# The order list of latent attention extended over the first part of the joining stage

## The chip, the cores and the metric

The kernel runs as one program on one core of a Trainium2 chip. The figure of merit is the device time of one execution in microseconds (us). The kernel before was timed three times: 1685.85, 1685.1 and 1686.39 us, median 1685.85. A further execution was recorded by the hardware profiler, and every duration below comes from that one recording. The engines are named as in the profile: PE (matrix products), PEld (its weight loads), DVE (vector), ACT (scalar), POOL (general purpose, here mostly the issuer of stores) and SP (issuer of most loads). L12 is line 12 of the kernel that is spoken of; the changed kernel's lines from 917 on have other numbers.

## The reference

One step of an encoder layer, for a prompt of 1024 rows and a sample of 32 rows that also sees a cache of 512 rows, at a width of 1024:

```
h = rms_norm(x) * (1 + scale1) + shift1
q-latent, kv-latent, rope key, SB q/k/v, gate A, gate B = split(h @ w_in)
o_A = mla_attend(...)        # latent attention, 8 heads of 64, softmax, block-causal mask of 64 rows
o_B = sb_attend(...)         # stick-breaking attention, 8 heads of 64
merged = sigmoid(gate A) * (o_A @ w_proj_a) + sigmoid(gate B) * (o_B @ w_proj_b)
x = x + gate1 * rms_norm(merged @ w_out)
x = x + gate2 * rms_norm(conv_ffn(rms_norm(x) * (1 + scale2) + shift2))
```

The change concerns the end of `mla_attend` and the beginning of `o_A @ w_proj_a` in `merged`.

## The kernel before

**Precision.** Each fp32 operand of a large product is cut into a high and a low part. `hi` (L68) writes the high part on ACT, `lo` (L71) subtracts it on DVE, and `mm3` (L75, L76, L77) issues three matmuls for each product: high by high, high by low, low by high.

**Stages.** Normalised input, combined projection, stick-breaking attention, latent attention, joining (`merged` and `w_out`), and the feed-forward part follow each other. All activations are kept transposed, so that a tile has 128 features as partitions and up to 1056 rows (1024 and 32) as columns.

**Latent attention.** The eight heads are treated as four pairs, 0 to 3. For each head there are four units of 256 query rows, each with two blocks of 128 rows. Scores go into banks `s`, are exponentiated into a tile `A` of 128 x 1056, normalised there, and turned block by block through a bank `tr` into high and low parts: `PTh`/`PTl`, or `ptd` (one fixed pair of tiles) for the diagonal block. The products with the values run into a bank `pv` (L820). Its two halves are copied (`o<-pv` on ACT, L792) and added (`o<-pv,o` on DVE, L794). The outputs of pairs 0 to 2 are stored to `oa` in DRAM and those of pair 3 are split straight into a tile `V`.

**The order list.** What PE, ACT and DVE do in this stage follows a list written out by hand, `ORDER_M`, which `mla_attend` executes token by token. A token's digit is the pair, and its letter the step: S scores, M m n maximum, E exponential, R reciprocal, C or c normalising (DVE or ACT), T turning, h v high and low part of what was turned, V products with the values, o p the copy and the addition of the output, Y one step of the sample's attention, q r the split of pair 3's outputs. In `3T5.2`, 5 is the unit (4 and above: the pair's second head, counted backwards) and 2 the block. Tokens without a digit belong to gate B's projection (`proj_b`): Q e l its operand, U W w its weights, f one product (three matmuls of 264 columns) into a bank `mm`, and G the store of a finished bank, that is an ACT copy to a tile `nat` (L1889) and a transfer issued by POOL into `pbd` in DRAM (L1890). There are 32 such stores. Inside the listed part the three engines keep exactly this order; POOL and SP are not in the list and issue their transfers in an order that the scheduler derives.

**After the list.** The rows of pairs 1, 2 and 0 are loaded back from `oa` into tiles `big` (L1678, SP) and split into `QH`/`QL`, `KH`/`KL`, `QH`/`QL`. The weights for the joining stage's first two feature tiles (m = 0 and 1) are loaded and split, fifteen products with pairs 1, 2 and 0 run into five banks (m = 0 into mm, mm, s and m = 1 into s, s), and an ACT instruction on one column calls for the sigmoid's table (L1694), placed behind the last exponential. These steps are outside the list, so the scheduler puts them among and behind the list's last tokens. The fourth part of these products (pair 3, tile `V`) and everything else of the joining stage follows in `stage_merge`, which loads gate rows (`t<-gd` L2004, `t<-pbd` L2010) and `w_out` (L2027).

**Tile slots.** A tile of a tag is taken from a ring of a few buffers. Who writes a tile waits until the buffer's earlier reader is done, so an ACT copy into `nat` waits until the transfer that reads the same buffer has landed.

Of the kernel before, what the change touches and what calls it, by code (L numbers as in the profile page):

```python
# [17 lines left out]
P = 128  # L18
D = 1024
KT = 8  # L20
TP = 1024
TS = 32
T = TP + TS
NB = 352
PAST = 512
KS = PAST + TS
# [6 lines left out]
BIG = 1056  # L33
# [11 lines left out]
class K:  # L45
# [777 lines left out]
    def sb_weights(self, pieces, w):  # L823
# [76 lines left out]
        2v6.0 3n0.0 2c7.0 f 2y 3S1.0 3E0.0 2V6.0 3E0.1 G 2T7.0 3S1.1 f4 3S2.0b 3Y 3R0.0 2H 3c0.0 U 3R0.1 3M1.0  # L900
        3C0.1 2L 3n1.0 3M1.1 2g 2h7.0 2o6 3E1.0 3R1.0 W 3S2.0a 3c1.0 3Y 2v7.0 2p6 2V7.0 2b 3n1.1 3E1.1 3T0.0
        3M2.0b w 3R1.1 3Y 3M2.0a 3m2.0 3h0.0 3Y 2o7 3E2.0a 3S2.1a 3E2.0b G 3C1.1 3v0.0 f 3Y 2p7 3S2.1b 3s2.0 3Y
        3M2.1b 3M2.1a 3V0.0 3m2.1 3Y 3T1.1 3o0 3E2.1b 3T1.0 3h1.1 3h1.0 f 3v1.1 3Y f 3E2.1a f 3v1.0 3Y 3s2.1
        3R2.0 3Y 3S3.0a 3p0 3c2.0 f 3q f2 3V1.1 3R2.1 3S3.0b 3C2.1 3Y 3T2.1 3h2.1 3Y 3M3.0b 3Y f 3S3.1b 3V1.0
        3M3.0a 3m3.0 3Y 3v2.1 3T2.2 3E3.0b 3Y 3S3.1a 3E3.0a 3o1 3Y 3M3.1b 3S4.0b 3h2.2 W 3r 3M3.1a 3m3.1 3E3.1b
        3p1 3v2.2 3Y 3T2.0 w 3S4.0a 3M4.0b 3s3.0 3E3.1a 3R3.0 3S4.1a 3Y 3h2.0 3M4.0a 3m4.0 3s3.1 3c3.0 3E4.0b
        3v2.0 3V2.2 3S4.1b 3V2.1 3R3.1 3C3.1 3q 3T3.3 3Y 3E4.0a G 3T3.2 3V2.0 G 3M4.1b 3M4.1a 3h3.3 3h3.2 3v3.3
        3Y 3m4.1 3r 3s4.0 3T3.1 3o2 3p2 3E4.1a 3v3.2 3E4.1b 3Y 3s4.1 3h3.1 3R4.1 3V3.3 3R4.0 3V3.2 3C4.1 3c4.0
        3v3.1 3q 3Y 3T3.0 3T4.3 3V3.1 3S5.0a 3h3.0 f 3v3.0 3T4.2 3V3.0 3h4.3 3Y 3h4.2 3M5.0a 3v4.3 3o3 3S5.1b
        3T4.1 3S5.0b 3h4.1 3Y 3p3 3v4.2 3M5.0b 3V4.3 f 3Y 3V4.2 3m5.0 3v4.1 f 3r 3E5.0b 3Y 3E5.0a 3T4.0 3S5.1a  # L910
        3M5.1b 3s5.0 3Y 3R5.0 3M5.1a 3h4.0 3S6.1 3m5.1 3Y 3E5.1a 3E5.1b 3c5.0 3v4.0 3Y 3M6.1 3q 3Y 3S6.0 3s5.1
        3S7.1 3R5.1 3n6.1 3E6.1 3C5.1 3T5.2 3h5.2 3M6.0 3n6.0 3Y 3M7.1 3E6.0 3n7.1 3v5.2 3V4.1 3R6.1 3R6.0 3c6.0
        3Y 3C6.1 3V4.0 3T5.1 3o4 3h5.1 3r 3T5.0 3h5.0 3E7.1 f 3p4 3S7.0 3V5.2 3v5.1 3v5.0 G f 3M7.0 3q 3T6.1
        3h6.1 3n7.0 3R7.1 3r 3v6.1 3E7.0 3V5.1 3V5.0 3R7.0 3o5 3T6.0 3h6.0 f2 3c7.0 f 3p5 3C7.1 G 3v6.0 3V6.1
        3T7.0 3h7.0 3V6.0 f 3o6 f 3v7.0 f 3p6 f 3q 3V7.0 3r G 3o7 3p7 3q f3 3r f 3q 3r G
# [240 lines left out]
    def stage_sb(self):  # L1156
# [50 lines left out]
        fill = self.gates()  # L1207
        E = mybir.EngineType
        for p in range(4):
# [203 lines left out]
    def stage_mla(self):  # L1413
        nc, a = self.nc, self.a

        O = self.Op = self.tc.alloc_tile_pool(name="mlo", bufs=2, side="right", reuse_waits="tile")
        M = self.tc.alloc_tile_pool(name="mla", bufs=2, side="right", reuse_waits="tile")
# [7 lines left out]
        K0 = [O.tile([P, T], F32R, name=self.nm(n), bufs=1) for n in ("KH", "KL")]  # L1425
# [152 lines left out]
        raw = load_values(0)  # L1578
# [8 lines left out]
        def key_rows(i):  # L1587
# [20 lines left out]
        o3, sample = [], []  # L1608
# [49 lines left out]
        def shared(k):  # L1658
# [3 lines left out]
                latents.append(self.mla_sample_latents())  # L1662
            next(latents[0])

        E = mybir.EngineType
# [6 lines left out]
        q = lambda: [self.tl(O, [P, T], F32R, g) for g in ("QH", "QL")]  # L1672
        q0, q1 = q(), q()
        self.xh, self.xl = zip(q1, q0, K0, o3)
        ks = (1, 2, 0)
        for k in ks:
            f = self.tl(self.At, [P, BIG], F32, "big")
            nc.sync.dma_start(f, self.oad[k])  # L1678
            self.hi(self.xh[k], f)
            self.lo(self.xl[k], f, self.xh[k])  # L1680
        self.pa = []
        raw = self.tl(M, [P, 2, KS], F32, "KSm")
        raw = [self.w_proj_a(m, raw[:, m, :512]) for m in range(2)] + [self.w_proj_a(2)]
        self.w2 = raw[2]
        for m, tags in enumerate(("mm mm s", "s s")):
            h, l = self.split_proj(raw[m])
            self.pa.append((h, l, [self.bank(g) for g in tags.split()]))
            for ps, (c0, n) in zip(self.pa[m][2], self.BLK[::-1]):
                for k in ks:
                    self.mm3(ps[:, :n], h[:, k], l[:, k], self.xh[k][:, c0 : c0 + n], self.xl[k][:, c0 : c0 + n], k == 1, False)  # L1690

        z = self.tl(self.sm, [P, 1], F32, "ss")
        with self.tc.issue_after(self.exp.ins):
            nc.scalar.activation(z, self.epsc, AF.Sigmoid)  # L1694
        M.release()
        self.Lp.release()
        self.sm3.release()
# [133 lines left out]
    def proj_b(self, M, AB):  # L1831

        nc, a = self.nc, self.a
        HB = HC // 2
        TILES = ((0, 1), (1, 2), (3, 1), (4, 1), (5, 2), (7, 1))
        raw, w, ps, obs, fs, done = [], [], [], [], [], [0, 0, 0, 0, 0]
# [48 lines left out]

        def store():
            m, c0, x = ps.pop(0)
            g = self.tl(self.At, [P, 512], F32, "nat")[:, :HB]
            nc.scalar.copy(g, x)  # L1889
            nc.gpsimd.dma_start(self.pbd[m, :, c0 : c0 + HB], g)  # L1890
# [273 lines left out]
    HB = ((0, 256), (256, 272))  # L2164
# [557 lines left out]
```

## Time and profile before

| | |
|---|---|
| Median of three runs | 1685.85 us (1685.1 to 1686.39) |
| Profiled execution | 1686.9 us, of which the recorded span is 1685.1 us |
| Granted TensorE clock over the span | 0.994 |
| PE busy | 1643.0 us (97%) |
| DVE busy | 1268.6 us (75%) |
| ACT busy | 1008.5 us (60%) |
| POOL busy | 299.7 us (18%) |

Latent attention's pair 3 stands at about 763 to 827 us of the span, and the first products of the joining stage begin at 827.3 us. "Busy" is time in which an engine has an instruction under way; matmuls overlap, so a row of PE may start before the row above has ended. In a timeline row the first number is the start and the second the duration in us, and what stands in brackets is the idle time ahead of the instruction and what ended it. A row with SPq or POOLq is the issue of a transfer and not the transfer.

### The profile page before, as it was taken

The numbers are of one execution on the slowest core, as the hardware profiler recorded it, in microseconds if no ns is written. First come the engines' busy times: TensorE is split into PE (matmuls) and PEld (weight loads), VectorE is DVE, ScalarE is ACT, GpSimd is POOL, SyncE is SP. The second block draws the span as 40 slices with busy tenths as digits, with TensorE's granted clock in tenths as the row PEclk, the third lists the DMA queues.
The fourth block names the chain that finished last, engine by engine and source line by source line (L and its number), as shares of the span: only waits on it lengthen the run. The fifth ranks groups of instructions, "written<-read, shape, count | busy, mean of one in ns | idle before, by whom it ended". The sixth has DMA issues, their size and how long they took to land. (4 is left out here: it accounts for less than half of the span.)

```text
span 1685.1 us, 30257 instructions
## 1 busy us (share of the span) xinstructions
PE 1643.0 (97%) x11592; PEld 1506.5 (89%) x11592; DVE 1268.6 (75%) x2140; ACT 1008.5 (60%) x1945; POOL 299.7 (18%) x581
## 2 busy tenths in 40 slices
PE   5999999999999999999999999999999999999997
PEld 2899999999998889998888799999999999877885
DVE  4865698989883688987766789878777778787455
ACT  4544697878874488887762675545444444454442
POOL 4113312111210221111000222212111112200013
PEclk8999999999999999999999999999999999999999
DMA  9336885566632533222374523333333333797643
GB/s 357 107 108 199 276 250 164 161 193 181 180 117 50 163 99 97 80 88 66 132 235 135 184 88 123 133 127 105 128 126 97 133 129 105 244 325 243 197 140 122
DMA packets 194145, 260.62 MB, mean 155 GB/s; under 512 B 23374, under 2 KB 132304, under 8 KB 193936
## 3 DMA queue, kind: packets, MB, share of 16 engines
q1 hardware_dynamic: 172944, 198.50, 37.8%
q0 software_dynamic: 20688, 59.56, 10.0%
q8 instruction: 91, 1.49, 0.4%
q10 hardware_dynamic: 368, 0.63, 0.1%
q14 instruction: 54, 0.44, 0.1%
HBM read 191.11 MB, written 67.82 MB: 154 GB/s over the span
## 5 line engine op out<-in xcount | busy, mean ns | idle before, releaser
L68 ACT ACTIVATE wh<-wr 128x1024 fp32r<-128x1024 f32 (+2 forms) x151 | 130.1, 864 | 229.2 <-PE s L2176 85.4
L71 DVE TENSOR_TENSOR wl<-wr,wh 128x1024 fp32r<-128x1024 f32 (+2 forms) x151 | 148.3, 985 | 78.6 <-ACT wh L68 78.4
L75 PE MATMUL mm<-hh,wh 128*128 128x352 f32 x456 | 152.3, 334 | 0.4 <-DVE hh L332 0.4
L76 PE MATMUL mm<-hl,wh 128*128 128x352 f32 x456 | 148.1, 325 | 0.4 <-DVE hl L333 0.3
L77 PE MATMUL mm<-hh,wl 128*128 128x352 f32 x456 | 148.1, 325 | 0.0
L2175 PE MATMUL mm<-T,wh 128*128 128x256 f32 (+1 forms) x376 | 108.3, 288 | 0.0
L2177 PE MATMUL mm<-T,wl 128*128 128x256 f32 (+1 forms) x376 | 107.3, 286 | 0.4 <-DVE wl L71 0.2
L2176 PE MATMUL mm<-T,wh 128*128 128x256 f32 (+1 forms) x376 | 106.8, 284 | 0.0
L2175 PE MATMUL s<-T,wh 128*128 128x256 f32 (+1 forms) x348 | 99.4, 286 | 0.0
L2177 PE MATMUL s<-T,wl 128*128 128x256 f32 (+1 forms) x348 | 99.4, 286 | 0.0
L2176 PE MATMUL s<-T,wh 128*128 128x256 f32 (+1 forms) x348 | 98.9, 284 | 0.0
L71 DVE TENSOR_TENSOR wl<-S,wh 128x1024 fp32r<-128x1024 f32 (+1 forms) x55 | 59.2, 1078 | 51.5 <-ACT wh L68 49.9
L75 PEld LDWEIGHTS mm<-hh,wh 128*128 128x128 f32 x456 | 86.3, 189 | 3.8 <-issue 2.1
L76 PEld LDWEIGHTS mm<-hl,wh 128*128 128x128 f32 x456 | 86.4, 190 | 2.3 <-DVE hl L333 0.9
L2316 DVE SCALAR_TENSOR_TENSOR u<-u,c,u 128x1058 f32<-128x1058 f32 x68 | 87.1, 1317 | 1.9 <-ACT u L2313 0.7
L806 PE MATMUL tr<-c,A 128*128 128x128 f32 x576 | 86.7, 272 | 0.0
L77 PEld LDWEIGHTS mm<-hh,wl 128*128 128x128 f32 x456 | 86.1, 189 | 0.6 <-issue 0.4
L68 ACT ACTIVATE wh<-S 128x1024 fp32r<-128x1024 f32 (+1 forms) x55 | 51.8, 943 | 48.2 <-PE s L2176 13.4
L2175 PE MATMUL tr<-T,wh 128*128 128x272 f32 (+1 forms) x272 | 77.9, 287 | 0.0
L2177 PE MATMUL tr<-T,wl 128*128 128x272 f32 (+1 forms) x272 | 77.8, 286 | 0.0
L2176 PE MATMUL tr<-T,wh 128*128 128x272 f32 (+1 forms) x272 | 77.4, 285 | 0.0
L68 ACT ACTIVATE PTh<-tr 128x512 fp32r<-128x512 f32 x96 | 57.0, 599 | 27.3 <-PE tr L806 22.9
(768 smaller groups left out, 5812.0 us busy)
## 6 DMA issues: line engine op xcount, KB each, us to landing
wr<-in_w_up_dram SPq DMA_DIRECT2D x44, 512.0 KB, 4.0
dr<-in_w_down_dram SPq DMA_DIRECT2D x43, 512.0 KB, 5.2
wr<-in_w_in_dram SPq DMA_DIRECT2D x33, 512.0 KB, 6.5
A<-in_w_ada_dram SPq DMA_DIRECT2D x32, 512.0 KB, 5.8
wr<-gdn SPq DMA_DIRECT2D x30, 512.0 KB, 4.4
gdn<-u POOLq DMA_DIRECT2D x23, 512.0 KB, 5.2
gd<-nat POOLq DMA_DIRECT2D x48, 176.0 KB, 3.4
t<-gd SPq DMA_DIRECT2D x16, 528.0 KB, 5.3
```

What stands on the lines that cost most here:

```text
L68: self.nc.scalar.activation(out, in_, AF.Identity, scale=scale)
L71: return self.nc.vector.tensor_tensor(out, full, hi.bitcast(F32), ALU.subtract)
L75: m(ps, lh, rh, start=start, stop=False)
L76: m(ps, lh, rl, start=False, stop=False)
L77: self.pe = m(ps, ll, rh, start=False, stop=stop).ins
L806: self.nc.tensor.transpose(tr[:, (2 * s + q) * P : (2 * s + q + 1) * P], at[q][:, b * P : b * P + P], self.idt)
L2175: m(ps[:, :n], w[0][:, k], x[0][:, k, c], start=first and k == 0, stop=False, skip_group_check=True)
L2176: m(ps[:, :n], w[0][:, k], x[1][:, k, c], start=False, stop=False, skip_group_check=True)
L2177: i = m(ps[:, :n], w[1][:, k], x[0][:, k, c], start=False, stop=k == 3, skip_group_check=True)
L2316: nc.vector.scalar_tensor_tensor(y, u[:, w : w + YW], self.cvT[:, w, cc : cc + 1], y, ALU.mult, ALU.add)
```

## The change

The steps that stood behind the list become tokens of it, under a new digit 7: `7h` and `7l` split the loaded rows (three each), `7W` and `7w` split the joining stage's weights (two each, m = 1 ahead of m = 0), `7P` is one of the fifteen products (fifteen tokens), and `7z` is the one-column sigmoid that calls for the table. The list's part for pair 3 is written anew from `3S1.1` on, with the same steps in another order, and the pair-7 tokens stand in its last part. The products of m = 1 come first and take banks s and s, then m = 0 takes s, mm, mm. The three loads of rows are written where the first `7h` stands. Finally, the last four of the 32 stores of gate B's projection copy into a tile `A` and no longer into a `nat`. The engines execute the same numbers of instructions of every kind as before.

```diff
+        3M7.1 3n7.1 f G 3T6.1 3n7.0 3V5.1 f 7h 7h 7l 7h 3E7.1 3h6.1 f 3E7.0 7l 3V5.0 7P 7l 3o5 3q 3T6.0 3R7.0 G
+        f 3h6.0 f2 7P 3v6.1 3p5 7P 3c7.0 7W 7P 3R7.1 7P 3V6.1 G 3C7.1 3T7.0 3h7.0 3v6.0 7P 3V6.0 7w 3r 7P 7P 3q
+        7P 3o6 3v7.0 3p6 3V7.0 3r 7z 7P 3o7 7P 3q 3p7 3r 7P 7P 7P 3q 3r 7P
...
+        def rows():
+            q = lambda: [self.tl(O, [P, T], F32R, g) for g in ("QH", "QL")]
+            q0, q1 = q(), q()
+            self.xh, self.xl = zip(q1, q0, K0, o3)
+            for k in ks:
+                fs.append(self.tl(self.At, [P, BIG], F32, "big"))
+                nc.sync.dma_start(fs[-1], self.oad[k])
...
+        def merge_weights(i):
...
+            m = 1 - todo[2 + i]
...
+                self.pa[m] = [self.tl(self.W, [P, 1024], F32R, g)[:, :512] for g in ("wh", "wl")]
+                self.hi(self.pa[m][0], raw[m])
...
+            for m, tags in ((1, "s s"), (0, "s mm mm")):
...
+        last = dict(h=lambda: merge_rows(0), l=lambda: merge_rows(1), W=lambda: merge_weights(0), w=lambda: merge_weights(1),
+                    P=lambda: next(products), z=lambda: nc.scalar.activation(self.tl(self.sm, [P, 1], F32, "ss"), self.epsc, AF.Sigmoid))
...
-            self.mla_attend({p: lambda p=p: one(p) for p in range(4)}, {8: second, 9: lambda k: first[k]()}, shared)
+            self.mla_attend({p: lambda p=p: one(p) for p in range(4)},
+                            {7: lambda k: last[k](), 8: second, 9: lambda k: first[k]()}, shared)
...
-        for m, tags in enumerate(("mm mm s", "s s")):
-            h, l = self.split_proj(raw[m])
...
-        with self.tc.issue_after(self.exp.ins):
-            nc.scalar.activation(z, self.epsc, AF.Sigmoid)
...
-            g = self.tl(self.At, [P, 512], F32, "nat")[:, :HB]
+            done[5] += 1
+            g = self.tl(self.At, *(([P, 512], F32, "nat") if done[5] < 29 else ([P, TP], F32, "A")))[:, :HB]
```

In the rows below a name ends in its tile's number, and all numbers of the rewritten part differ between the two kernels.

On ACT, at the end of latent attention before the change, the table load stands directly behind the last exponential, and the splits of loaded rows (`KH<-big`, `QH<-big`) stand between copies and splits of the outputs:

```order
L1694 ACT_TABLE_LOAD
L1694 ACTIVATE ss_1793_10571<-c_4_76 128x1
L792 COPY o_1761_10399<-pv_1757_10364 64x256
L68 ACTIVATE PTh_1763_10406<-tr_1762_10401 128x512
L971 ACTIVATE A_1753_10356<-A_1753_10356,sum_1755_10358 128x128
L1889 COPY nat_1765_10421<-mm_1759_10374 128x264
L68 ACTIVATE KH_1044_6987<-big_1780_10500 128x1056
L68 ACTIVATE ptd_1042_6982<-tr_1767_10430 128x384
L792 COPY o_1769_10443<-pv_1766_10425 64x256
L68 ACTIVATE V_1582_9577<-o_1761_10399 64x256
L68 ACTIVATE QH_1777_10494<-big_1781_10504 128x1056
L1889 COPY nat_1771_10463<-mm_1768_10439 128x264
```

On ACT after the change, at the corresponding place, a store's copy (into `A`) stands ahead of the three row splits, which follow each other, and the last two exponentials (`A,sum<-s,mx,lat`) and another store's copy stand behind them:

```order
L1915 COPY A_1765_10406<-mm_1742_10306 128x264
L68 ACTIVATE QH_1767_10421<-big_1771_10425 128x1056
L68 ACTIVATE KH_1044_6987<-big_1772_10427 128x1056
L68 ACTIVATE QH_1769_10423<-big_1773_10429 128x1056
L963 ACTIVATE A_1760_10382,sum_1762_10384<-s_1763_10385,mx_1761_10383,lat_955_6225 128x256
L68 ACTIVATE ptd_1042_6982<-tr_1766_10409 128x384
L963 ACTIVATE A_1755_10368,sum_1757_10370<-s_1758_10371,mx_1756_10369,lat_955_6225 128x128
L792 COPY o_1776_10452<-pv_1764_10395 64x256
L68 ACTIVATE V_1582_9577<-o_1754_10364 64x256
L1915 COPY A_1780_10463<-mm_1759_10377 128x264
L68 ACTIVATE PTh_1778_10460<-tr_1777_10455 128x512
L972 ACTIVATE A_1755_10368<-A_1755_10368,sum_1757_10370 128x128
```

The row splits moved ahead of the last exponentials, as one block of three, and the two store copies that stand around them use `A` tiles.

Also on ACT after the change, the table load stands nearly at the list's end, between the last two copies of outputs:

```order
L68 ACTIVATE ptd_1042_6982<-tr_1786_10505 128x384
L68 ACTIVATE V_1582_9577<-o_1776_10452 64x256
L792 COPY o_1788_10531<-pv_1784_10496 64x256
L1713 ACT_TABLE_LOAD
L1713 ACTIVATE ss_1790_10541<-c_4_76 128x1
L792 COPY o_1792_10547<-pv_1789_10535 64x256
L68 ACTIVATE V_1582_9577<-o_1788_10531 64x256
L68 ACTIVATE V_1582_9577<-o_1792_10547 64x256
```

It moved behind the copy of the last output but one.

On PE before the change, the joining stage's products (352 columns) begin where the last product of gate B's projection (264 columns) has ended, in banks mm and s:

```order
L75 MATMUL mm_1773_10470<-ObH_1412_8746,wh_1050_6993 128x264
L76 MATMUL mm_1773_10470<-ObL_1413_8747,wh_1050_6993 128x264
L77 MATMUL mm_1773_10470<-ObH_1412_8746,wl_1051_6994 128x264
L75 MATMUL mm_1786_10517<-QH_1775_10492,wh_1784_10513 128x352
L76 MATMUL mm_1786_10517<-QL_1776_10493,wh_1784_10513 128x352
L75 MATMUL s_1788_10519<-QH_1775_10492,wh_1784_10513 128x352
L76 MATMUL s_1788_10519<-QL_1776_10493,wh_1784_10513 128x352
```

On PE after the change the first of these products stands among attention's value products and turnings, with more of both still to come:

```order
L820 MATMUL pv_1764_10395<-PTh_1749_10349,V_1424_8795 128x256
L820 MATMUL pv_1764_10395<-PTl_1750_10350,V_1424_8795 128x256
L75 MATMUL s_1775_10447<-QH_1767_10421,wh_1746_10335 128x352
L76 MATMUL s_1775_10447<-QL_1768_10422,wh_1746_10335 128x352
L77 MATMUL s_1775_10447<-QH_1767_10421,wl_1747_10336 128x352
L806 MATMUL tr_1777_10455<-c_1_70,A_1737_10292 128x128
L806 MATMUL tr_1777_10455<-c_1_70,A_1726_10243 128x128
```

The joining products moved from behind attention's last product to between its turnings and value products. PE's order is the same in both kernels up to about 763 us of the span and again from the place that stood at about 853 us.

More of the change, by code (lines that the diff above doesn't have):

```diff
@@ new lines @@
+        3V0.0 3Y 3s2.0 3M2.1b 3m2.1 3o0 3T1.0 2b 3E2.1b 3T1.1 3E2.1a 3p0 3Y 3h1.1 f 3R2.0 3s2.1 3h1.0 3Y f 3v1.1
+        3R2.1 3c2.0 3C2.1 3V1.1 3Y f 3S3.0b 3v1.0 3T2.2 3Y 3h2.2 3V1.0 3M3.0b 3Y f 3v2.2 3o1 3T2.1 3S3.0a f 3q
+        3Y 3p1 3h2.1 3V2.2 W 3M3.0a 3S3.1b 3m3.0 3Y 3v2.1 3T2.0 3r 3Y 3M3.1b 3E3.0a 3E3.0b 3S3.1a 3S4.0a 3Y
+        3h2.0 3M3.1a 3Y 3m3.1 3M4.0a 3q 3E3.1a 3s3.0 3S4.0b f 3R3.0 3c3.0 3E3.1b 3S4.1b G 3v2.0 3Y 3M4.0b 3m4.0
+        3s3.1 3E4.0a 3R3.1 3E4.0b 3Y 3C3.1 3Y 3S4.1a w 3T3.3 3M4.1b 3V2.1 3h3.3 3M4.1a 3T3.2 3h3.2 3Y 3m4.1
@@ new lines @@
+        3V2.0 3v3.2 3E4.1a 3Y 3o2 3E4.1b 3T3.1 3v3.3 3s4.0 3p2 3r 3h3.1 3V3.3 3S5.1b f 3V3.2 3Y 3v3.1 3s4.1
+        3R4.1 3R4.0 3Y 3T3.0 f 3Y f 3V3.1 3h3.0 3Y 3c4.0 3Y 3C4.1 3S5.0a 3S5.0b 3Y 3q 3v3.0 3M5.0b 3V3.0 3Y
+        3M5.0a 3T4.3 3h4.3 3o3 3m5.0 3Y G 3E5.0b 3M5.1b 3S5.1a 3E5.0a 3v4.3 3T4.2 3p3 3r 3Y 3q 3Y 3M5.1a 3s5.0
+        3m5.1 3S6.1 3h4.2 3r 3v4.2 3V4.3 3R5.0 3E5.1a f 3E5.1b 3Y 3T4.0 3M6.1 3c5.0 3s5.1 3h4.0 3n6.1 3V4.2
+        3R5.1 3T4.1 3S6.0 3C5.1 3E6.1 G 3v4.0 f2 3M6.0 3T5.2 f 3n6.0 3h4.1 f 3E6.0 3h5.2 3R6.1 3v4.1 7W 3V4.1
@@ L1663, in shared, with merge_rows @@
             next(latents[0])
+        ks, fs, raw, self.pa, todo = (1, 2, 0), [], [], [None, None], [0] * 6
+        def rows():
[5 more added lines that the diff above has]
+                nc.sync.dma_start(fs[-1], self.oad[k])
+        def merge_rows(i):
+            if not fs:
+                rows()
+            k, f = ks[todo[i]], fs[todo[i]]
+            todo[i] += 1
+            if i:
+                self.lo(self.xl[k], f, self.xh[k])
+            else:
+                self.hi(self.xh[k], f)
@@ new lines, in merge_weights @@
+        def merge_weights(i):
+            if not raw:
+                x = self.tl(M, [P, 2, KS], F32, "KSm")
+                raw[:] = [self.w_proj_a(m, x[:, m, :512]) for m in range(2)] + [self.w_proj_a(2)]
+                self.w2 = raw[2]
+            m = 1 - todo[2 + i]
+            todo[2 + i] += 1
+            if i:
+                h, l = self.pa[m][:2]
+                self.lo(l, raw[m], h)
+            else:
+                self.pa[m] = [self.tl(self.W, [P, 1024], F32R, g)[:, :512] for g in ("wh", "wl")]
+                self.hi(self.pa[m][0], raw[m])
@@ new lines, in merge_products @@
+        def merge_products():
+            for m, tags in ((1, "s s"), (0, "s mm mm")):
+                h, l = (x.rearrange("p (k c) -> p k c", k=4) for x in self.pa[m])
+                banks = []
+                self.pa[m] = h, l, banks
+                for g, (c0, n) in zip(tags.split(), self.BLK[::-1]):
+                    banks.append(self.bank(g))
+                    for k in ks:
+                        self.mm3(banks[-1][:, :n], h[:, k], l[:, k], self.xh[k][:, c0 : c0 + n], self.xl[k][:, c0 : c0 + n], k == 1, False)
+                        yield
@@ L1665, in stage_mla @@
+        products = merge_products()
+        last = dict(h=lambda: merge_rows(0), l=lambda: merge_rows(1), W=lambda: merge_weights(0), w=lambda: merge_weights(1),
+                    P=lambda: next(products), z=lambda: nc.scalar.activation(self.tl(self.sm, [P, 1], F32, "ss"), self.epsc, AF.Sigmoid))
         E = mybir.EngineType
         with self.tc.manual_schedule(engines={E.PE, E.Activation, E.DVE}):
-            self.mla_attend({p: lambda p=p: one(p) for p in range(4)}, {8: second, 9: lambda k: first[k]()}, shared)
+            self.mla_attend({p: lambda p=p: one(p) for p in range(4)},
+                            {7: lambda k: last[k](), 8: second, 9: lambda k: first[k]()}, shared)
@@ L1668, in stage_mla @@
         for _ in split(self.osm[:, 3], slice(0, P), slice(TP, T)):
             pass
[L1672 to L1682, printed above, removed]
@@ L1683, in stage_mla @@
-        raw = [self.w_proj_a(m, raw[:, m, :512]) for m in range(2)] + [self.w_proj_a(2)]
-        self.w2 = raw[2]
-        for m, tags in enumerate(("mm mm s", "s s")):
-            h, l = self.split_proj(raw[m])
[L1687 to L1690, printed above, removed]
@@ L1835, in proj_b @@
         TILES = ((0, 1), (1, 2), (3, 1), (4, 1), (5, 2), (7, 1))
[L1836 removed]
+        raw, w, ps, obs, fs, done = [], [], [], [], [], [0, 0, 0, 0, 0, 0]
         def fetch():
```

21 lines of the change are left out of this document (4 added, 17 removed).

## The prediction

> **What bounds the kernel now.** I read the page first, for which engine carries the span:
>
> ```profile
> PE 1643.0 (97%) x11592; PEld 1506.5 (89%) x11592; DVE 1268.6 (75%) x2140; ACT 1008.5 (60%) x1945; POOL 299.7 (18%) x581
> ```
>
> PE is busy for 97% of 1685.1 us, and the change neither adds nor removes a matmul. So it can only gain what PE idles in the rewritten stretch. PE's order differs from about 763 us on and is the same again from what stood at 853 us; I therefore asked for busy time by stretches (PE, PEld, DVE, ACT, POOL, then clock and DMA share) and for PE's waits in the same window:
>
> ```profile
> 821.00:827.30 6.30, 5.25 (x39) 4.93 (x40) 5.51 (x10) 5.82 (x12) 1.55 (x10) 1.00 1.02 396
> 827.30:836.00 8.70, 7.56 (x48) 7.26 (x47) 3.37 (x5) 4.33 (x6) 0.54 (x1) 1.00 0.44 160
> ...
> sum 82.20, PE 78.00 PEld 69.76 DVE 60.12 ACT 60.98 POOL 6.91; mean PE 15.60 PEld 13.95 DVE 12.03 ACT 12.20 POOL 1.38
> ```
> ```profile
> PE pv L820 <- DVE o L794: 2.9, 4, 1.1
> PE mm L75 <- ACT nat L1889: 1.1, 1, 1.1
> ```
>
> The five stretches of 764 to 846.2 us add up to 82.20 us, with PE busy for 78.00. The waits have two names only. The timeline of PE shows them one by one, with the idle time in brackets:
>
> ```profile
> 766.98 0.72 PE L820 MATMUL pv<-ptd,V 128*128 128x256 f32 x4 [0.37 <-DVE o L794]
> ...
> 804.18 0.74 PE L820 MATMUL pv<-ptd,V 128*128 128x256 f32 x4 [0.78 <-DVE o L794]
> ...
> 821.34 0.75 PE L820 MATMUL pv<-ptd,V 128*128 128x256 f32 x4 [1.07 <-DVE o L794]
> ...
> 825.26 0.74 PE L820 MATMUL pv<-ptd,V 128*128 128x256 f32 x4 [0.71 <-DVE o L794]
> ...
> 829.27 0.43 PE L75 MATMUL mm<-QH,wh 128*128 128x352 f32 x1 [1.14 <-ACT nat L1889]
> ```
>
> The first value product of a unit needs the only bank `pv` back, which the copy and the addition of the previous output must have read. The idle times are 0.37 + 0.78 + 1.07 + 0.71 + 1.14 = 4.07 us: that is the ceiling, 0.24% of the time. What held them up is seen on ACT and DVE:
>
> ```profile
> 801.40 1.10 ACT L68 ACTIVATE QH<-big 128x1056 fp32r<-128x1056 f32 x1
> 802.38 0.61 ACT L68 ACTIVATE PTh<-tr 128x512 fp32r<-128x512 f32 x1
> 803.02 0.37 ACT L792 COPY o<-pv 64x256 f32<-64x256 f32 x1
> ...
> 818.94 1.28 ACT L1694 ACT_TABLE_LOAD   x1
> 820.23 0.20 ACT L1694 ACTIVATE ss<-c 128x1 f32<-128x1 f32 x1
> 820.46 0.36 ACT L792 COPY o<-pv 64x256 f32<-64x256 f32 x1
> ...
> 828.84 0.38 ACT L1889 COPY nat<-mm 128x264 f32<-128x264 f32 x1 [1.09 <-DMA pbd<-nat]
> ```
> ```profile
> 820.86 0.43 DVE L794 TENSOR_TENSOR o<-pv,o 64x256 f32<-64x256 f32 x1 [1.72 <-ACT o L792]
> ...
> 825.57 1.26 DVE L71 TENSOR_TENSOR QL<-big,QH 128x1056 fp32r<-128x1056 f32 x1
> ```
>
> A row split of 1.10 us stands ahead of the output copy at 803.02, and the table load ahead of that at 820.46. The last wait is another thing: the copy at 828.84 sat 1.09 us until an earlier store out of its `nat` buffer had landed, and PE waited for the bank which that copy empties.
>
> **The change, part by part.** *Removed.* I walked PE, ACT and DVE by hand through the new order with the durations of before's rows. The output copies now stand behind short instructions, and of the five waits 0.15 us remain (the value product near 766 us, whose `ptd` low part is late); the others vanish, with margins of 0.35 us and more. So the full 4.07 us is taken as removed, and what remains or comes new is charged below.
>
> *Table load.* It stands behind the last output copy but one. From the value products that this copy reads to the end of the last unit's, PE has nine joining matmuls at 0.16 us (rows below) and four value products at about 0.12: 1.9 us. In that time ACT copies (0.36) and loads the table (1.28 + 0.20): 1.84, just ready for the last copy. The last copy, the addition (0.43) and the split of the output follow:
>
> ```profile
> 826.53 0.41 ACT L68 ACTIVATE V<-o 64x256 fp32r<-64x256 f32 x1
> ```
> ```profile
> 827.21 0.42 DVE L71 TENSOR_TENSOR V<-o,V 64x256 fp32r<-64x256 f32 x1
> ```
>
> Together 0.36 + 0.43 + 0.41 + 0.42 = 1.6 us, against 18 further joining matmuls (2.9 us) ahead of the first that reads tile V. Nothing is charged; without the nine matmuls the load would cost up to 1.48.
>
> *Moved matmuls.* A product behind a turning costs more than one behind a product:
>
> ```profile
> 756.76 0.60 PE L806 MATMUL tr<-c,A 128*128 128x128 f32 x4
> 757.11 0.37 PE L75 MATMUL mm<-ObH,wh 128*128 128x264 f32 x1
> 757.32 0.28 PE L76 MATMUL mm<-ObL,wh 128*128 128x264 f32 x1
> 757.44 0.28 PE L77 MATMUL mm<-ObH,wl 128*128 128x264 f32 x1
> ```
> ```profile
> 830.98 0.33 PE L75 MATMUL mm<-KH,wh 128*128 128x352 f32 x1
> 831.14 0.32 PE L76 MATMUL mm<-KL,wh 128*128 128x352 f32 x1
> ```
>
> The first takes 757.32 − 757.11 = 0.21 us, the next 0.12, so 0.09 us for each seam. In the changed stretch there were 16 such seams and now there are 19: 3 x 0.09 = 0.27 us lost.
>
> *Row loads, row splits, stores.* Here lies what the new order may cost. POOL issues the sample's rows and the gate stores, SP the loads behind them:
>
> ```profile
> 815.08 0.54 POOL L1811 DMA_DIRECT2D oa<-os  x1 [20.46 <-DVE os L1809]
> 817.70 0.54 POOL L1890 DMA_DIRECT2D pbd<-nat  x1 [2.08 <-ACT nat L1889]
> ```
> ```profile
> 816.88 0.84 SPq L1678 DMA_DIRECT2D big<-oa  x2
> 817.77 0.90 SPq L2004 DMA_DIRECT2D t<-gd  x2
> ```
>
> The rows' load needs the sample's write, 816.88 − 815.08 = 1.8 us later, and the gate rows follow on the same queue. From then on the DMA engines are full: the share in the first row of stretches is 1.02. The store issued at 817.70 meets that, and the next one too. Issue to landing of these transfers, from the DMA views of 817 to 818.5 and 822 to 823 us, then least, median and longest of the four stores of 815 to 831 us, and of the four gate-row loads (528 KB, L2004) issued between 815 and 821 us:
>
> ```profile
> pbd<-nat POOLq DMA_DIRECT2D x1, 132.0 KB, 6.0
> ```
> ```profile
> pbd<-nat POOLq DMA_DIRECT2D x1, 132.0 KB, 6.5
> ```
> ```profile
> DMA to landing us min/median/max: 3.5/5.1/6.5
> ```
> ```profile
> DMA to landing us min/median/max: 6.4/8.0/9.7
> ```
>
> Let T be the start of the second long run of f32 matmuls of the sample's attention, in before:
>
> ```profile
> 808.43 2.97 PE L1795 MATMUL tr<-A,VSm 128*128 128x128 f32 x20
> ```
>
> In the new order, by my walk, the sample's write leaves at T + 6.0 and the first store out of an `A` tile at T + 8.8, that is 2.8 us later (2.6 before). I take 6.0 us for its landing, from the nearest row, the store in the same position: T + 14.8. ACT reaches the next store's copy, which takes the same `A` buffer, at T + 13.3 and sits 1.5 us. Behind it on ACT stand the three row splits, 0.98 us from start to start (801.40 to 802.38), with three of 1.26 on DVE. The first joining product needs the first pair of them by T + 17.0, where PE gets; they are ready at T + 17.3: 0.3 us lost. The second store then leaves at T + 15.2 and lands at T + 20.6 (5.4 us, between the median 5.1 and 6.0), while ACT comes to the third copy at T + 20.25. What is queued behind that copy, the normalising of the last block, makes a turning about 0.5 us late. Other joining products have margins of 0.65 to 2 us, since PE has gate products and turnings in between.
>
> The landing is the unknown cost. Its bounds are 3.5 us, the least in this stretch, with which ACT waits for neither store (both terms zero), and 9.7, the longest of the four times larger gate-row loads beside it. Beyond 6 us both waits grow, one us each per us: PE's loss is about 2L − 11 (1 us at L = 6, 8.4 at 9.7).
>
> By the Trainium skill, page "DMA: Bandwidth & Descriptors", section "Anatomy of one DMA — SWDGE (gpsimd) path", a transfer issued by POOL takes about 2.0 us and then its bytes at 436 GB/s, an estimate of 2.3 us for 132 KB. The rows of this stretch, at full DMA engines, show 6.0 and 6.5. By the page the sum below would be without 0.3 and 0.5, and the time about 1682.4.
>
> *Joining stage.* The `w_out` load of m = 1 is issued later against the gate rows than before (its place on SP is swapped with a load of `pbd`), by about 7.6 us in my walk; its split has about 2 us of margin left, so nothing is charged. Were that gone, each us late would be one us of PE.
>
> *Sum.* 4.07 − 0.27 − 0.15 − 0.3 − 0.5 = 2.85, less 0.25 for a wait that a hand walk does not see (an estimate: one more margin of about 0.35 us that row-to-row scatter uses up): 2.6 us. The profiled execution took 1686.9 us (span 1685.1 and 1.8 around it) and would come to 1684.3. It lies 1.05 us above the median of 1685.85, so the median becomes 1683.2 us.
>
> **The rivals.** *A: the stores land in time.* If L is 5 or less the two store waits vanish, and 4.07 − 0.27, less up to 0.4 for small waits, is gained: 1682.0 to 1682.5. For it speaks the least and median landing of 3.5 and 5.1, and that the stretch has the same loads; against it, that the store in the same position took 6.0.
>
> *B: the stores chain.* Two `A` copies in a row wait, each for the landing of the store before, and all row splits and two exponentials are queued behind. PE breaks even where 2L − 11 = 3.8, at L = 7.4, and is over 0.2% (3.4 us, which is also about what a measurement of this kernel can tell from no change) slower from L = 9.1. At 9.7 the loss is 8.4 − 3.8 = 4.6 us: 1690.4. For it: the same stretch has loads of up to 9.7, and the gate-row loads follow the row loads closer than in before. Against it: no store there took over 6.5.
>
> *C: the waits only move.* ACT was busy for 5.82 of 6.30 us and DVE 5.51 in the stretch where the waits were. With three row splits in a block (2.9 us on ACT, 3.8 on DVE) an output copy or a turning may be late by 0.7 to 1.1 us, the sizes of the waits of before, at three to five places. Then 2.1 to 5.5 of the 3.8 us are lost again: 1684.2 to 1687.6. Against it: PE has joining products, 0.48 us each, to run in between.
>
> **How the numbers follow.** The forecast (1682.6 to 1685.0) gets 0.47, A 0.26, C 0.12, B 0.15. Faster by over 0.2% needs a gain above 3.4 us, nearly the ceiling, which only A gives: 0.26. Slower by over 0.2% is B: 0.15. The forecast and C are the same within 0.2%: 0.59. The range starts at 1681.6, the ceiling without seams (1685.85 − 4.07 = 1681.8) and 0.2 of scatter, and ends at 1687.5, where C ends; it leaves out B and a little.
>
> **What would show it.** Right: the table load behind the last output copies with no PE idle after it; no PE wait on the addition at 804, 821 and 825 us; one ACT wait of about 1.5 us on a `pbd<-A` transfer ahead of the block of three row splits, and a smaller one behind; store landings near 6. Wrong: both ACT waits gone (A); each above 3 us and PE waiting for QL or for the last turning (B); PE waits named `o L794` or `tr` of 0.7 and more at new places (C). The forecast also fails if the joining stage, 830 to 860 us, shows a wait on `w_out` or on a gate row that it had not.

## The result and the profile after

The changed kernel takes 1681.11 us (median of eight runs, 1680.17 to 1682.39), the kernel before beside it 1685.88 (eight runs, 1685.1 to 1687.52). The ratio is 0.9970 with a 95% interval of 0.9961 to 0.9979: 4.8 us or 0.28% faster. That is beyond the ceiling of 4.07 us that the prediction read off the profile, and beyond its range. The profiled execution took 1682.39 us, with a span of 1680.6.

The page's first part, and PE's waits of 755 to 860 us. Before, this window had the five waits of two names that the prediction shows, and behind the changed part one of 0.44 us at 853.31:

```profile
PE 1642.6 (98%) x11592; PEld 1506.9 (90%) x11592; DVE 1268.5 (75%) x2140; ACT 1007.7 (60%) x1945; POOL 303.2 (18%) x581
```
```profile
PE pv L820 <- DVE ptd L71: 0.2, 1, 0.2
```

PE's busy time is the same as before to 0.4 us. One wait is left. The first value products of the units, which stood behind the additions before, now start without a bracket, apart from the second product of the one near 767 us:

```profile
767.06 0.28 PE L820 MATMUL pv<-ptd,V 128*128 128x256 f32 x1
767.58 0.62 PE L820 MATMUL pv<-ptd,V 128*128 128x256 f32 x3 [0.24 <-DVE ptd L71]
...
810.36 0.63 PE L820 MATMUL pv<-ptd,V 128*128 128x256 f32 x4
...
818.52 0.63 PE L820 MATMUL pv<-ptd,V 128*128 128x256 f32 x4
...
825.31 0.63 PE L820 MATMUL pv<-ptd,V 128*128 128x256 f32 x4
```

ACT at the end of the stretch has the block of row splits, one wait for a store, and the table load ahead of the last output copy:

```profile
817.95 0.38 ACT L1915 COPY A<-mm 128x264 f32<-128x264 f32 x1
818.21 1.11 ACT L68 ACTIVATE QH<-big 128x1056 fp32r<-128x1056 f32 x1
...
824.27 0.38 ACT L1915 COPY A<-mm 128x264 f32<-128x264 f32 x1 [0.80 <-DMA pbd<-A]
...
827.77 1.28 ACT L1713 ACT_TABLE_LOAD   x1
829.07 0.20 ACT L1713 ACTIVATE ss<-c 128x1 f32<-128x1 f32 x1
829.29 0.36 ACT L792 COPY o<-pv 64x256 f32<-64x256 f32 x1
```

POOL and SP show when the stores and the loads left, and the DMA views of 813.5 to 814.3 us and of the store at 818.62 how long the first two took to land (2.0 and 5.6 us):

```profile
810.93 0.54 POOL L1836 DMA_DIRECT2D oa<-os  x1 [4.07 <-DVE os L1834]
813.75 0.54 POOL L1916 DMA_DIRECT2D pbd<-A  x1 [2.28 <-ACT A L1915]
818.62 0.54 POOL L1916 DMA_DIRECT2D pbd<-A  x1 [4.33 <-ACT A L1915]
```
```profile
814.57 0.83 SPq L1674 DMA_DIRECT2D big<-oa  x2
```
```profile
pbd<-A POOLq DMA_DIRECT2D x1, 132.0 KB, 2.0
```
```profile
DMA to landing us min/median/max: 5.6/5.6/5.6
```

**A measure for one stretch.** Whole times scatter by some us from run to run, so the experiments below are also compared by the stretch of PE that the change rewrites: from the gate product ahead of the second group `mm<-lat,wh` to the first `pv<-dh,gs` of the joining stage. PE has the same number of matmuls in it in all these kernels. Before and after:

```profile
760.08 0.29 PE L75 MATMUL mm<-ObH,wh 128*128 128x264 f32 x1
...
846.19 0.64 PE L1935 MATMUL pv<-dh,gs 128*32 128x256 f32 x8
```
```profile
761.37 0.28 PE L75 MATMUL mm<-ObH,wh 128*128 128x264 f32 x1
...
842.12 0.64 PE L1961 MATMUL pv<-dh,gs 128*32 128x256 f32 x8
```

That is 86.11 us before and 80.75 after: 5.36 us less, each from one recording. Ahead of the stretch, where PE's order is the same in both, the profiled execution of after was 1.29 us later, and behind it 0.43 us shorter (1685.1 − 846.19 = 838.91 against 838.48): scatter, which makes 4.5 us of the span out of 5.36.

**Where 5.36 us come from when the brackets show 4.07.** A bracket counts idle time from the end of the instruction before, and the profile models the ends of matmuls. But PE's instructions normally overlap, so that a start costs more than its bracket when it has to wait. The rows around the first wait of before (the waiting row at 766.98, with 0.37 in its bracket, stands in the prediction), and the same two kinds of rows without a wait in the profile of after:

```profile
766.22 0.39 PE L1624 MATMUL s<-KH,QL 128*128 128x320 f32 x1
...
767.53 0.49 PE L806 MATMUL tr<-c,A 128*128 128x128 f32 x3
```
```profile
802.94 0.39 PE L1625 MATMUL s<-KH,QL 128*128 128x320 f32 x1
803.17 0.31 PE L1620 MATMUL s<-KH,QH 128*128 128x320 f32 x1
...
810.83 0.28 PE L75 MATMUL mm<-ObH,wh 128*128 128x264 f32 x1
```

Without a wait the score matmul gives way after 0.23 us, though it ends after 0.39: 0.16 us of overlap. The four value products take 810.83 − 810.36 = 0.47. With the wait the two take 767.53 − 766.22 = 1.31 us, not 0.70: 0.61 us lost under a bracket of 0.37. Worked out in this way the other four lost 1.06, 1.34, 0.99 and 1.40. The five come to 5.40 us, each 0.24 to 0.28 above its bracket: 0.16 of overlap, and 0.08 to 0.11 because the matmul behind the waiting one starts late too. For the last of the five this is seen in before's rows, where the next matmul starts 0.26 us behind the waiting one of 829.27 and not 0.16:

```profile
829.53 0.33 PE L76 MATMUL mm<-QL,wh 128*128 128x352 f32 x1
```

The Trainium skill, page "TensorE: Matmul & The Clock Gate", sections "Single matmul latency" and "Back-to-back issue gap", gives for a bf16 matmul at the full clock a latency of (398 + N)/2.4 ns and a spacing of N/2.4 + 2.5 ns; the difference is an estimate of 0.16 us whatever N is. The rows above agree (0.39 − 0.23). The one wait left in after costs 0.24 + 0.27 = 0.51, so the waits with brackets account for 4.89 of the 5.36 us.

Before also had starts that waited without a bracket. The largest stood behind four turnings at 768.58. It came 0.72 us behind the start of the turnings, where 0.35 is usual, with an idle time of 0.12 us (768.58 − 767.86 − 0.60). Before and after:

```profile
767.86 0.60 PE L1738 MATMUL tr<-c,big 128*128 128x128 f32 x4
768.58 0.44 PE L1619 MATMUL s<-KH,QH 128*128 128x384 f32 x1
```
```profile
768.37 0.60 PE L1763 MATMUL tr<-c,big 128*128 128x128 f32 x4
768.72 0.39 PE L1620 MATMUL s<-KH,QH 128*128 128x320 f32 x1
```

That is 0.37 us late. Two more such places of before, at 765.78 (0.11) and at 822.45 and 822.67 (0.18 together), make it 0.66, and none of the three is left in after. So after has 5.40 + 0.66 − 0.51 = 5.55 us less of waiting, and the rest of its stretch is 0.19 us longer.

### The profile page after: what moved, and what is told of

The parts are those of the page before. It is cut to its first block, busy times and chain, and to the rows that moved or that the text cites. A ratio compares the mean times of both kernels' runs of the same rounds, so it can differ in the third digit from the quotient of the medians.

```text
span 1680.6 us, 30263 instructions
## 1 busy us (share of the span) xinstructions
PE 1642.6 (98%) x11592; PEld 1506.9 (90%) x11592; DVE 1268.5 (75%) x2140; ACT 1007.7 (60%) x1945; POOL 303.2 (18%) x581
## 5 line engine op out<-in xcount | busy, mean ns | idle before, releaser
L2332 POOL COPY c<-u 128x2 f32<-128x2 f32 x44 | 26.9, 611 | 264.9 <-DVE u L2278 229.1
```

## The experiments

The theory after the result: the change took five waits of PE away and left one, each worth its bracket and about 0.27 us; and the stores cost nothing because the first one left ahead of the loads. The rivals: a wait costs what its bracket shows and the rest came from elsewhere; the A tiles, or the listing of the tail as such, bring the gain. All runs in one table, brackets with their number:

| run | stretch (start, end) | brackets | median, us | ratio to before, 95% |
|---|---|---|---|---|
| before | 86.11 (760.08, 846.19) | 4.07 (5) | 1685.88 | |
| changed kernel | 80.75 (761.37, 842.12) | 0.24 (1) | 1681.11 | 0.9961 to 0.9979 |
| copies_5 | 81.32 (761.60, 842.92) | 0.57 (2) | 1681.57 | 0.9962 to 0.9985 |
| copies_9 | 82.94 (762.11, 845.05) | 2.15 (2) | 1682.94 | 0.9975 to 0.9993 |
| copies_13 | 86.52 (761.05, 847.57) | 3.78 (2) | 1686.34 | 0.9994 to 1.0014 |
| nat_stores | 80.73 (759.30, 840.03) | 0.26 (1) | 1681.48 | 0.9965 to 0.9985 |
| a_stores_only | 85.00 (762.45, 847.45) | 2.96 (4) | 1685.47 | 0.9985 to 1.0003 |
| store_held | 86.72 (760.16, 846.88) | 2.83 (3) | 1685.33 | 0.9985 to 1.0005 |
| order_only | 83.52 (759.56, 843.08) | 2.47 (3) | 1683.00 | 0.9976 to 0.9993 |
| order_m1_first | 83.45 (761.17, 844.62) | 1.93 (3) | 1682.69 | 0.9969 to 0.9988 |
| tail_appended | 95.36 (759.65, 855.01) | 9.40 (3) | 1694.60 | 1.0033 to 1.0064 |
| table_last | 83.56 (759.36, 842.92) | 1.93 (4) | 1682.82 | 0.9971 to 0.9989 |
| table_early | none (see below) | | 1681.43 | 0.9960 to 0.9981 |
| table_early_2 | 81.43 (760.05, 841.48) | 0.56 (2) | 1681.69 | 0.9967 to 0.9987 |
| ptd_early | 80.70 (760.10, 840.80) | none | 1679.56 | 0.9947 to 0.9972 |
| ptd_and_nat | 80.40 (758.70, 839.10) | none | 1680.73 | 0.9968 to 0.9986 |

### What a wait costs

In the changed kernel one output copy was repeated, so that PE's next use of bank `pv` comes late by a set amount (5, 9 or 13 copies):

```diff
-                    nc.scalar.copy(res[n][r], pv[n][q, :256])
+                    for _ in range(self.again):
+                        nc.scalar.copy(res[n][r], pv[n][q, :256])
...
+                self.again = 5 if p == 3 and k == "o" and n == 2 else 1
```

> The changed kernel with the output copy of unit 2 of pair 3 (ACT at 796.68 us, which waited for PE there) done five times over instead of once, so that the addition, and with it the next use of bank pv at 798.60, comes about 4 x 0.385 = 1.55 us later. The slack there is about 1.05 us, so PE waits about 0.5. It measures what a wait of PE costs. Theory (a wait costs its idle time in brackets and about 0.28 us more, 0.16 for the overlap of two matmuls that is lost and 0.12 for a slower start): PE shows a wait of about 0.3 and the stretch grows from 80.75 by 0.6, in all by the brackets plus 0.28 for each wait. Rival (a wait costs what its brackets show): it grows by the brackets alone.

> As the run with five copies, with nine: the addition about 3.1 us late, so PE waits about 2.0. Theory: the stretch grows by the sum of the brackets and 0.28 for each wait, so by about 1.9 + 0.28 = 2.2 us if there is one wait, to 82.9, and the time by about 2.2. Rival: by the brackets alone, 1.9.

PE's waiting rows with five copies, and with nine:

```profile
799.39 0.74 PE L822 MATMUL pv<-ptd,V 128*128 128x256 f32 x4 [0.31 <-DVE o L796]
```
```profile
801.49 0.74 PE L822 MATMUL pv<-ptd,V 128*128 128x256 f32 x4 [1.91 <-DVE o L796]
```

The stretch grew by 0.57 under a bracket of 0.31 and by 2.19 under one of 1.91: 0.26 and 0.28 above it, for a short wait as for one six times as long. The rival falls.

> As the runs with five and nine output copies (stretch 81.32 and 82.93), with thirteen: one single wait of PE of about 3.45 us in brackets. In the run with the held store two waits of 1.71 and 0.86 us within 3.2 us were followed by 6.5 us with the TensorE clock granted at 0.50. Theory (the clock is cut when PE has idled for long enough within a few us, in one piece or two): the clock falls to 0.5 behind the wait too, and the stretch is 80.75 + 0.3 + 3.45 + 0.28 + about 3, so 87 to 88. Rival (the held store cut the clock for another reason, and a wait costs its brackets and 0.28): 84.3 to 84.8, clock 1.00 throughout.

Here the growth was 5.77 us under a bracket of 3.53. By bracket and 0.28 it would be 3.81. Of the other 1.96 some 1.7 lie in the clock, which stood at 0.50 for 3.4 us behind the wait and so cost half of that (columns as in the stretches of the prediction, the clock third from the end), and nearly 0.3 in one late turning without a bracket near 831.1:

```profile
803.00:804.00 1.00, 1.00 (x7) 1.00 (x7) 0.93 (x5) 0.68 (x3) 0.00 (x0) 0.72 0.00 0
804.00:805.00 1.00, 1.00 (x7) 1.00 (x6) 0.56 (x5) 0.56 (x2) 0.00 (x0) 0.50 0.00 0
...
806.00:807.00 1.00, 1.00 (x7) 1.00 (x7) 0.84 (x2) 1.00 (x2) 0.00 (x0) 0.57 0.00 0
```

The theory's clock cut is there, and it cost less than expected (1.7 us and not 3).

### The stores

```diff
-            done[5] += 1
-            g = self.tl(self.At, *(([P, 512], F32, "nat") if done[5] < 29 else ([P, TP], F32, "A")))[:, :HB]
+            g = self.tl(self.At, [P, 512], F32, "nat")[:, :HB]
```

> The changed kernel with its last four stores back in nat tiles. Theory (the A tiles gain nothing: with the new order no copy comes to its nat buffer before the store two ahead has landed, and the second store, 5.6 us under full DMA engines, holds no copy up any more): no ACT wait on a store, stretch 80.5 to 81.0, time 1680.5 to 1681.7, the same as the changed kernel. Rival (the A tiles are what removed the wait of 1.14 us on the copy at 828.84): that wait is back, stretch 82 and time 1682.5.

The stretch is 80.73 against 80.75: in the new order the A tiles are worth nothing, going by one recording of each. The opposite single edit, A tiles in the kernel before:

> The kernel before with the store change alone: the last four stores copy into A tiles. Theory (the copy at 828.84 waited for a nat buffer; the first A tiles are free, and the last one waits for the first of the four stores, which left early): the wait of 1.14 us on PE is gone, the other four stay, the stretch falls by 1.4 to 84.7, time 1684.2 to 1684.8. Rival (the fourth copy waits as long for its A buffer): unchanged, 1685.5 to 1686.3.

The wait of 1.14 us is gone from the names, but the stretch fell by 1.11 and not by 1.4; the time did not move measurably. The row that had carried the wait (829.27 before), and the one ahead of it:

```profile
830.10 0.32 PE L76 MATMUL s<-QL,wh 128*128 128x352 f32 x1
830.52 0.43 PE L75 MATMUL mm<-QH,wh 128*128 128x352 f32 x1
```

830.52 − 830.10 = 0.42, where 0.16 is usual: 0.26 us late with no bracket at all. The matmul before had ended only 0.10 us earlier (830.10 + 0.32), which is too short for a bracket in these views.

Then the first of the four stores was held back on POOL in the changed kernel:

```diff
+            for _ in range(3 if done[5] == 29 else 0):
+                nc.gpsimd.tensor_copy(g, g)
```

> The changed kernel with the first of the last four stores held back on POOL: after the ACT copy POOL copies the tile three times onto itself before it issues the transfer. In the changed kernel this store left at 813.75, 0.82 us ahead of the first row load (814.57), and landed in 2.0 us; the next one, at 818.62 under full DMA engines, took 5.6. Theory (it landed soon because it left ahead of the loads): held back by 1.5 us or more it takes 4.5 to 6.5, ACT waits 2 to 4 us ahead of the block of row splits, PE waits for QL, the stretch grows by 1.5 to 4 us. Rival (a store of 132 KB lands in 2 to 3 us as long as few stores are under way): ACT waits under 0.8 us and the stretch stays within 0.3 of 80.75.

Issue of the row loads and of the store, and what ACT and PE then waited for:

```profile
813.06 0.81 SPq L1674 DMA_DIRECT2D big<-oa  x2
```
```profile
813.97 0.55 POOL L1918 DMA_DIRECT2D pbd<-A  x1 [0.30 <-POOL A L1917]
```
```profile
DMA to landing us min/median/max: 6.7/6.7/6.7
```
```profile
820.73 0.38 ACT L1915 COPY A<-mm 128x264 f32<-128x264 f32 x1 [3.89 <-DMA pbd<-A]
```
```profile
PE mm L75 <- ACT A L1915: 1.7, 1, 1.7
PE s L76 <- DVE QL L71: 0.9, 1, 0.9
```

0.9 us behind the loads and not 0.8 ahead of them, the store took 6.7 us and not 2.0. ACT sat 3.89 us. The stretch grew by 5.97, more than expected: by 2.57 more in brackets and two more waits (0.56), and by some 2.8 that remain, with the clock at half in this profile too. It had fallen when the second wait (0.86 us, from 822.58) began:

```profile
821.16:822.58 1.42, 1.42 (x8) 1.09 (x8) 0.45 (x1) 1.42 (x2) 0.54 (x1) 1.00 1.01 408
822.58:823.44 0.86, 0.00 (x0) 0.00 (x0) 0.86 (x2) 0.86 (x2) 0.00 (x0) 0.53 1.06 427
...
827.00:829.00 2.00, 2.00 (x9) 2.00 (x8) 1.68 (x3) 1.49 (x4) 0.74 (x2) 0.50 0.19 68
```

### The order and the listing of the tail

The kernel before with the new order of pair 3 but the joining steps outside the list. Of the list's last lines:

```diff
-        3T7.0 3h7.0 3V6.0 f 3o6 f 3v7.0 f 3p6 f 3q 3V7.0 3r G 3o7 3p7 3q f3 3r f 3q 3r G
...
+        f 3h6.0 f2 3v6.1 3p5 3c7.0 3R7.1 3V6.1 G 3C7.1 3T7.0 3h7.0 3v6.0 3V6.0 3r 3q
+        3o6 3v7.0 3p6 3V7.0 3r 3o7 3q 3p7 3r 3q 3r
```

> The kernel before with the new order of pair 3 alone: the steps of the joining stage stay outside the list, and the stores keep their nat tiles. Theory (the waits on the output additions were taken away by the order of pair 3, and neither the listing of the tail nor the A tiles matter): the five waits of before are gone here too, the stretch of PE from the gate product ahead of the second mm<-lat,wh group to the first pv<-dh,gs (86.11 us before, 80.75 after) comes to 80.5 to 81.3, and the time to 1681 to 1682. Rival (the listing of the tail gains it): a stretch of 83.5 or more and a time of 1683.5 to 1686.

```profile
PE mm L75 <- ACT nat L1890: 1.3, 1, 1.3
PE tr L1788 <- ACT A L1790: 1.0, 1, 1.0
PE pv L820 <- DVE ptd L71: 0.3, 1, 0.3
```

This theory was wrong by half. The waits on the additions are gone, and 2.59 us with them, but two others stand in their place: the scheduler put a row split ahead of the sample's copy into A, and the first joining products into banks `mm`, which come free only with a store's copy. By elimination the list brings the other 2.77 us, since the A tiles brought nothing. With m = 1 first in the same kernel:

```diff
-        for m, tags in enumerate(("mm mm s", "s s")):
+        for m, tags in ((1, "s s"), (0, "s mm mm")):
```

> The run with the new order alone (tail unlisted, stretch 83.52) with one edit: the fifteen products are written with m = 1 first, into banks s and s, and then m = 0 into s, mm and mm, as in the changed kernel. Theory (of the 2.77 us that listing the tail is worth, 1.26 + 0.28 lie in the wait of the first products for a bank mm, which comes free only with a store's copy, and 0.95 + 0.28 in the row split that the scheduler puts ahead of the sample's copy): the first wait goes, the second stays, stretch 81.9 to 82.1, time 1682. Rival (the products are late for another reason, the row splits or weights): 83 to 83.6.

The wait for a bank `mm` went as expected, but a wait of 0.68 us on an addition came up, and the stretch stayed: 83.45. So the bank order alone isn't what the list adds. Listing is not it either without the places:

```diff
+        7h 7l 7h 7l 7h 7l 7W 7w 7W 7w 7z 7P 7P 7P 7P 7P 7P 7P 7P 7P 7P 7P 7P 7P 7P 7P
```

> The changed kernel's code with the old order of pair 3, and the tokens of the tail appended at the list's end (all splits, then the table load, then the fifteen products). Theory (it is the places that count): PE has nothing left but the joining products while three row splits of 0.98 us on ACT and 1.26 on DVE are made one after the other, the waits at 804, 821 and 825 us partly stay, and PE idles 4 to 7 us more: 1688 to 1693. Rival (being listed is what gains, wherever): 1681 to 1684.

PE waited 4.0 us for the splits behind each other, and 5.0 for a split of the next weights. The time rose by 9 us, a little beyond the expected range: 5.33 us more in brackets than before, and the clock stood at 0.50 for 6.8 us from within each of the two waits. The waits of the old order at 804, 821 and 825 us did not stay in part, as the theory had it, but went altogether, although pair 3 has its old order here. So in the old order it was the joining steps between the output copies, the row splits and the table load, that made them.

### The table load

The kernel before with the one-column sigmoid behind the last output copy:

```diff
-        with self.tc.issue_after(self.exp.ins):
+        with self.tc.issue_after(self.copied):
```

> The kernel before with one edit: the one-column sigmoid is placed behind the last output copy and not behind the last exponential. The scheduler then also puts one split of weights and seven joining matmuls earlier. Theory (the wait of 1.07 us in brackets at 821 cost 1.35): that wait is gone, and the ones at 825 and 829 change, the stretch being 80.3 plus the sum of the brackets plus 0.28 for each wait; with two waits left 82.5 to 84, time 1682.5 to 1684.5. Rival (the table load's place is worth nothing, the copy behind it waits for something else): 1685 to 1686.5.

The stretch fell by 2.55 us, with the waits at 821 and 825 gone and 0.38, 0.79, 0.44 and 0.33 us left. Since the scheduler moved joining products too, not all of it is the load's. The opposite edit, the token `7z` directly behind the last exponential in the changed kernel:

> The changed kernel with the table load moved from behind the last output copy but one to directly behind the last exponential, where it stands in the kernel before. Theory (what the load costs depends on what is queued behind it; here that is an output copy with about 1.5 us of margin and a normalising with about 1 us): PE waits 0.3 to 0.5 in brackets for the last turning, the stretch grows by 0.4 to 1.0 us. Rival (the load costs its whole 1.48 us on the path wherever it stands ahead of an output copy): it grows by 1.4 to 1.8.

The recorded execution of this run took 4126.31 us, for a reason that the record doesn't show, so that its profile is of no use. The other eight took 1678.53 to 1682.99. A second run gave a profile:

> The table load directly behind the last exponential in the changed kernel, once more, for its profile. Theory: PE waits 0.2 to 0.5 us in brackets for the last turning, the stretch grows from 80.75 by 0.4 to 1.0 us. Rival (the load costs its whole 1.48 us on the path): it grows by 1.4 to 1.8.

PE's waits in the second run:

```profile
PE tr L806 <- ACT A L972: 0.3, 1, 0.3
PE pv L820 <- DVE ptd L71: 0.3, 1, 0.3
```

The load itself kept its 1.28 and 0.20 us on ACT, and the stretch grew by 0.68: the wait for the last turning at 0.30 + 0.28, and 0.1 in small joins. What it costs is what is queued behind it.

### The wait that was left

One token moved in the changed kernel, so that the low part PE waits for at 767.58 is made ahead of another split:

```diff
-        3C0.1 2h7.0 3M1.0 2p6 3c0.0 w 2L 3n1.0 3Y 3E1.0 G 2v7.0 3M1.1 2V7.0 3T0.0 3h0.0 3v0.0 3Y 3S2.0a f 3n1.1
+        3C0.1 2h7.0 3M1.0 2p6 3c0.0 w 2v7.0 2L 3n1.0 3Y 3E1.0 G 3M1.1 2V7.0 3T0.0 3h0.0 3v0.0 3Y 3S2.0a f 3n1.1
```

> The changed kernel with one token moved: the low part of the diagonal block that PE waits for at 767.58 us (DVE, ptd) is taken ahead of the split of the key rows (KL, 0.68 us) which stood before it. Theory: the changed kernel's only wait in the stretch (0.24 in brackets, about 0.5 with the restart) goes, the stretch falls from 80.75 to 80.2 to 80.4, and the time by 0.5, to about 1680.6. Rival (the later KL makes PE wait as long at its next scores): unchanged within 0.15.

No wait of PE is left, and its start behind that place comes 0.51 us earlier; 0.16 is lost at once at the next scores, and 0.3 at the end in a few starts that are up to 0.11 late. There ACT waits longer for the same store, since it arrives earlier:

```profile
ACT A L1915 <- DMA pbd<-A: 1.1, 1, 1.1
```

> The run with the earlier ptd split (stretch 80.70) with the last four stores in nat tiles. Theory (waits shorter than the overlap of two matmuls show no bracket and cost all the same; the copy that waited 1.13 us for a store out of an A tile made three starts of PE late by 0.3 us in all): no ACT wait on a store, no late starts, stretch 80.25 to 80.45; time 1679.5 to 1681, within the scatter of the run before it. Rival (the late starts come from the order itself): 80.65 to 80.75.

80.40, as the theory has it: without that wait these starts are on time. Two edits beat the changed kernel by 0.35 us of the stretch. Their whole times (0.9947 to 0.9972 and 0.9968 to 0.9986) can't be told from the changed kernel's (0.9961 to 0.9979).

## Why the prediction was wrong, step by step

- **"So the full 4.07 us is taken as removed"** is the step that failed. The idle times in brackets were taken as the ceiling. The same five waits were worth 5.40 us, since each also breaks the overlap of two matmuls (0.16) and makes the next start late (0.08 to 0.11), and 0.66 us more stood in starts that waited without a bracket. With 5.40 for 4.07 the prediction's own sum is 3.9 and not 2.6 us, and its lowest bound, which was the ceiling too, falls from 1681.6 to 1680.3, below the measured time. The other parts of the miss are the 0.8 us charged for the stores, which cost nothing, and the 0.25 us for a wait that the walk does not see.
- **The remaining 0.15 us near 766 us**: the place and cause were right (a `ptd` low part that is late); it measured 0.24 in the bracket and 0.51 in all.
- **Row loads, row splits, stores (0.3 + 0.5 us)**: the first landing was mis-sized, 2.0 us for 6.0. The store left nearly where the walk had it (9.2 us behind T = 804.53, forecast 8.8), but the loads left 10.0 behind T, not 7.8: 3.64 us behind the sample's write and not 1.8. So the store was ahead of them. Why the load's issue took longer was not tried. The second landing (5.6 for 5.4) was right, and ACT's wait of 0.80 there is what the forecast called the smaller one; PE lost nothing by it.
- **Rival A** was what happened to the stores, and its gain was short for the same reason as the forecast's. **Rival B**'s mechanism is real: at a landing of 6.7 us its formula gives 2.4 us of loss. The held store lost 5.97, of which 3.1 are its waits and the rest came with the clock at half. **Rival C** did not come.
- **Moved matmuls (0.27 us)**: a product behind a turning still takes 0.21 (814.17 to 814.38, see below), and with all waits taken out, those without a bracket too, the stretch is 0.19 us longer. So the term was about right.
- **Table load, nothing charged**: right. It ran from 827.77 to 829.27 and the last copy followed at 829.29 without PE waiting. **Joining stage, nothing charged**: right, no wait on `w_out` or a gate row.
- The chances followed from the ceiling: "faster by over 0.2%" needed nearly all of 4.07 us, and had 0.26.

```profile
814.17 0.37 PE L75 MATMUL mm<-ObH,wh 128*128 128x264 f32 x1
814.38 0.28 PE L76 MATMUL mm<-ObL,wh 128*128 128x264 f32 x1
```

## What to carry to other kernels

On an engine whose instructions overlap, the idle time in a profile is less than what a wait costs: compare starts with the same two instructions where they don't wait. Here that was 0.24 to 0.28 us for each wait of PE, a third on top of the brackets, and 0.66 us stood in waits without a bracket. And when a small store leaves just ahead of a burst of loads or just behind it can matter: here 1.7 us in that order made 2.0 or 6.7 us of landing.

## What was not expected of the hardware

The granted TensorE clock fell to 0.50 after waits of very different length. With thirteen copies it did so for 3.4 us behind a single wait of 3.53 us. With the held store it did so for 6.8 us, and it fell as the second wait began, so behind one wait of 1.71 us alone. In the changed kernel's own recording it did so far ahead of the changed part, where PE's only wait between 500 and 532 us was one of 0.6 us that ended at 526.14:

```profile
523.90:527.30 3.40, 2.83 (x22) 2.58 (x22) 0.90 (x3) 0.95 (x2) 0.57 (x1) 1.00 0.00 0
527.40:530.70 3.30, 3.30 (x15) 3.18 (x15) 0.56 (x3) 1.17 (x2) 0.54 (x1) 0.50 0.04 10
```

Yet it stayed at 1.00 behind the single wait of 1.91 us with nine copies, and through the three of before (1.07, 0.71 and 1.14 within 9 us). So neither the length of one wait nor the sum of waits close together decides it in these runs, and what does stays open. The Trainium skill, page "TensorE: Matmul & The Clock Gate", section "What's actually happening", has the clock halved after about one idle window of 3.4 us. The wait of 3.53 us is of that length, but the ones of 1.71 and 0.6 us are shorter, and there the measurement decides.
